# Rotation of queries and keys: one PSUM bank each, four crosswise copies of 256 columns, and a planner that keeps a bank's readers apart

## The chip, the core and the metric

The kernel runs on one core of a Trainium2 chip. The metric is the device time of one execution in microseconds. Three executions of the kernel before took 576.04, 576.35 and 577.06 us.

## The reference

A decoder trunk of two layers works on 256 tokens of 1024 features in float32. Layer 0 is causal block attention with 16 heads of 64 (one block covers all tokens), layer 1 is dilated window attention with 12 heads in three groups. Each is followed by a squared-ReLU MLP of 4096, and each of the four parts ends in a layer norm of `alpha * x + f(x)`. What matters here is how the queries and keys are made:

```python
def apply_rotary(t, cos, sin):
    t1, t2 = jnp.split(t, 2, axis=-1)
    c = cos[None, :, None, :]
    s = sin[None, :, None, :]
    return jnp.concatenate([t1 * c - t2 * s, t2 * c + t1 * s], axis=-1)

...
    qkv = (x @ w_qkv).reshape(B, S, 3, H, dh)
    q = apply_rotary(qkv[:, :, 0], cos, sin) * (dh ** -0.5)
    k = apply_rotary(qkv[:, :, 1], cos, sin)
```

## The kernel before

**Precision and engines.** Every float32 operand is split into a high part (ScalarE, L316) and a low part (VectorE, L321), and a product is three TensorE matmuls: high by high, high by low, low by high. Weights come in tiles of 128 x 1024 through the SP queue into `raw`, and are split into `whi` and `wlo` (`load_w`). A split of 1024 columns takes 1.06 us on ScalarE and 1.22 us on VectorE.

**Pairs of heads.** Two heads fill 128 partitions. For each pair (eight in layer 0, six in layer 1) `proj_qk` projects q and k with 24 matmuls of 256 columns each (`mm_wstat`) into the two halves of one PSUM bank of the tag `acc`. There are four banks `acc` and four `tp`, eight in all. The first two pairs are projected from the staged input (`Stage.mms`, `NFIRST` = 4 projections) while it arrives.

**The rotation** (`rotate`) of such a bank: the feature rows are ordered so that the partner of a row lies 64 partitions away. ScalarE makes two crosswise copies (L544), each of 64 partitions and 512 columns, into the tile `b`. VectorE (L520) multiplies the bank by the cosines into `a`, multiplies `b` by the signed sines, and adds: three instructions of 512 columns. Then q is split into `qhi` and `qlo`, and k into `khi` and `klo` with a head mask (L556, L527).

**After the rotation.** `score` makes the scores in `tp` banks; VectorE masks them and takes the extreme (L591), ScalarE takes the exponential (L601), VectorE scales (L608), TensorE transposes (L615), ScalarE copies the transposed probabilities out of PSUM (`pt`, L623), and TensorE multiplies them with V. Output projection, layer norm and MLP follow.

**The order of the work** comes from a planner (`Plan`). The kernel only lists operations with an engine, a cost and their reads and writes. `order` first works out due times from behind, and then runs all engines forward in estimated time: on each engine it takes, among the operations that can start first, the one that is due first. A buffer of a tag is given to the operations in the order in which the kernel named them; a bank is free when its last operation is done. The resulting order is emitted, and semaphores make each instruction wait for those that it depends on. The emitted program also makes an instruction of ScalarE wait for one of VectorE that reads the same PSUM tile ahead of it in the order, and the other way round. The planner does not know of that wait: reads of one buffer are free of each other in it. A PSUM copy of n columns on ScalarE is put at

```python
    def act(n, aps=0, sbuf=False):
        return n / 1200 + (0.093 if sbuf else 0.055) + 0.093 * aps
```

and the crosswise copies at `act(512) + 0.1`; VectorE's products at `n / 960 + 0.07`.

Of the kernel before, what the change touches and what calls it, by code (L numbers as in the profile page):

```python
# [68 lines left out]
class Buf:  # L69


    def __init__(self, pool, shape, dtype, tag, name):
        self.pool, self.shape, self.dtype, self.tag, self.name = pool, shape, dtype, tag, name
        self.real = None
        self.state = {}
        self.left = 0
        self.held = False

    @property
    def t(self):  # L80
# [9 lines left out]
class Plan:  # L90
# [47 lines left out]
    def order(self):  # L138
        clock = {e: BEGIN[e] for e in ("PE", "SP")}
        bus = 0.0  # L140
        for o in self.ops:
            t = max([clock.get(o.eng, 0.0)] + [p.end + latency(p, o) for p in o.preds])
            o.end = t + o.cost
            if o.eng in clock:
                clock[o.eng] = o.end
            if o.xfer:
                bus = o.end = landed(t, bus, o.xfer)
            o.due = t - o.ahead if o.eng == "PE" else None
        t = clock["PE"]
        for o in reversed(self.ops):  # L150
            for q in o.succs:
                d = q.due - o.cost - latency(o, q)
                o.due = d if o.due is None else min(o.due, d)
            if o.due is None:
                o.due = t - o.early
        engines = sorted({o.eng for o in self.ops})
        free = {e: BEGIN[e] for e in engines}
        bus = 0.0
        cand = {e: [] for e in engines}
        slots = {tag: [0.0] * cap for tag, cap in self.caps.items()}  # L160
        done = []
        for o in self.ops:
            o.wait = len(o.preds)
            o.ready = 0.0
            if not o.wait:
                cand[o.eng].append(o)

        loads = [o for o in self.ops if o.eng == "SP"]

        def start_of(o):  # L170
            s = max(o.ready, free[o.eng])
            need = {}
            for b in o.bufs:
                if not b.held:
                    need.setdefault(b.tag, []).append(b)
            for tag, bs in need.items():
                q = self.queue[tag]
                spare = 0
                if {id(b) for b in q[: len(bs)]} != {id(b) for b in bs}:
                    if tag not in LOOSE:  # L180
                        return None
                    spare = 1
                if len(slots[tag]) < len(bs) + spare:
                    return None
                s = max(s, sorted(slots[tag])[len(bs) - 1])
            return s

        total = len(self.ops)
        while len(done) < total:
            best = None  # L190
            for e in engines:
                lst = [(start_of(o), o) for o in cand[e] if e != "SP" or o is loads[0]]
                lst = [x for x in lst if x[0] is not None]
                if not lst:
                    continue
                first = min(s for s, _ in lst)
                s, o = min((x for x in lst if x[0] <= first), key=lambda x: (x[1].due, x[1].n))
                if e in PATIENT:
                    worst = PATIENT[e]
                    now, ready = s, o  # L200
                    for s2, o2 in lst:
                        if now < s2 < now + ready.cost and o2.due < ready.due:
                            waits = max(s2 - o2.due, s2 + o2.cost - ready.due)
                            runs = max(now - ready.due, now + ready.cost - o2.due)
                            if runs - waits > worst:
                                worst, s, o = runs - waits, s2, o2
                if best is None or s < best[0]:
                    best = (s, o)
            assert best is not None
            s, o = best  # L210
            cand[o.eng].remove(o)
            if o.eng == "SP":
                loads.pop(0)
            for b in o.bufs:
                if not b.held:
                    slots[b.tag].remove(min(slots[b.tag]))
                    self.queue[b.tag].remove(b)
                    b.held = True
            cost = o.cost * 2 if o.eng == "PE" and s < PE_COLD else o.cost
            free[o.eng] = s + cost  # L220
            o.end = s + cost
            if o.xfer:
                bus = o.end = landed(s, bus, o.xfer)
            done.append((s, o.n, o))
            for b in o.bufs:
                b.left -= 1
                b.last = max(getattr(b, "last", 0.0), o.end + (PE_OUT if o.eng == "PE" else LAT))
                if not b.left:
                    slots[b.tag].append(b.last)
            for q in o.succs:  # L230
                q.wait -= 1
                q.ready = max(q.ready, o.end + latency(o, q))
                if not q.wait:
                    cand[q.eng].append(q)
        done.sort(key=lambda x: x[:2])
        return [o for _, _, o in done]
# [7 lines left out]


LOOSE = ("tp",)


LAYOUT = (
# [6 lines left out]
def tile_trunk(  # L256
# [87 lines left out]
    class Stage:  # L344
# [40 lines left out]
        def mms(self, ps, j):  # L385
            kt, hi, lo = self.kt, self.hi, self.lo
            c = slice(self.col(j), self.col(j) + P)
            i = (kt, self.part(j))
            last = kt == KT - 1 and j % 2 == 1
            for w, p, start, stop in ((hi, 0, kt == 0 and j % 2 == 0, False), (hi, 1, False, False), (lo, 0, False, last)):  # L390
                op(
                    "PE", 0.12,
                    lambda w=w, p=p, start=start, stop=stop: mm(
                        ps.t[:, j % 2 * S : j % 2 * S + S], w.t[:, c], xs[kt // 4].t[:, kt % 4, p, :], start, stop
                    ),
                    [(w, i)] + [(xs[kt // 4], (p, kt, m)) for m in range(2)], [ps],
                )
# [47 lines left out]
    def xk(kt, ms):  # L445
        return [(xs[kt // 4], (part, kt, m)) for part in range(2) for m in ms]

    def mm_wstat(ps, w, c0):
        def go_hi(kt):
            for part in range(2):  # L450
                mm(ps.t[:, c0 : c0 + S], w.hi.t[:, kt * P : (kt + 1) * P], xs[kt // 4].t[:, kt % 4, part, :], kt + part == 0, False)

        def go_lo(kt):
            mm(ps.t[:, c0 : c0 + S], w.lo.t[:, kt * P : (kt + 1) * P], xs[kt // 4].t[:, kt % 4, 0, :], False, kt == KT - 1)

        for kt in range(KT):
            op("PE", 0.24, lambda kt=kt: go_hi(kt), [(w.hi, 0)] + xk(kt, (0, 1)), [ps])
# [72 lines left out]
    def rotate(ps, ropet):  # L530
# [1 line left out]
        a = mk([P, 512], F32, "ta", 4)  # L532
        b = mk([P, 512], F32, "ta", 4)

        def pair(ap):
            return ap.rearrange("p (i s) -> p i s", i=2)

        def table(i):
            return ropet.t[:, i, :].unsqueeze(1).to_broadcast([P, 2, S])

        for h in range(2):
            op(
                "ACT", act(512) + 0.1,
                lambda h=h: nc.scalar.activation(b.t[64 * h : 64 * h + 64, :], ps.t[64 - 64 * h : 128 - 64 * h, :], AF.Copy),  # L544
                [ps], [(b, h)],
            )
        tt(512, lambda: pair(a.t), lambda: pair(ps.t), lambda: table(0), ALU.mult, [ps, ropet], [a])
        tt(512, lambda: pair(b.t), lambda: pair(b.t), lambda: table(1), ALU.mult, [b, ropet], [b])
        tt(512, lambda: a.t, lambda: a.t, lambda: b.t, ALU.add, [a, b], [a], ADD_ENG)
        q = mk([P, S], F32R, "qhi", 2), mk([P, S], F32R, "qlo", 2)  # L550
        split(S, lambda: a.t[:, :S], lambda: q[0].t, lambda: q[1].t, [a], [q[0]], [q[1]], sbuf=True)
        hi, lo = mk([P, 2, S], F32R, "khi", 2), mk([P, 2, S], F32R, "klo", 2)
        for h in range(2):
            op(
                "ACT", act(S, 1, True),
                lambda h=h: nc.scalar.activation(hi.t[:, h, :], a.t[:, S:], AF.Copy, scale=hm.t[:, h : h + 1]),  # L556
                [a, hm], [(hi, h)],
            )
            stt(
                S, 1, lambda h=h: lo.t[:, h, :], lambda: a.t[:, S:], lambda h=h: hm.t[:, h : h + 1],  # L560
                lambda h=h: f32(hi.t[:, h, :]), ALU.mult, ALU.subtract, [a, hm, (hi, h)], [(lo, h)],
            )
        return q, (hi, lo)

    def proj_qk(ws):
        ps = psum("acc")
        for i, w in enumerate(ws):
            mm_wstat(ps, w, i * S)
        return ps

    first_ps = [psum("acc") for _ in range(NFIRST // 2)]
    for st in stages:
        for j in range(NFIRST):
            st.mms(first_ps[j // 2], j)

    def score(ps, q, k, qc, kc, off=0):
        (qhi, qlo), (khi, klo) = q, k
# [268 lines left out]
    def layer0(between):  # L846
# [48 lines left out]

        def project(p):
            if 2 * p < NFIRST:
                return rotate(first_ps[p], ropes[0])
            return rotate(proj_qk([load_w(wqk0[2 * p + i - NFIRST]) for i in range(2)]), ropes[0])

        qk, sm = {}, {}
# [214 lines left out]
```

## Time and profile before

| | |
|---|---|
| median of three executions | 576.35 us |
| profiled execution | 576.27 us |
| its span, first to last instruction | 574.5 us |
| granted TensorE clock, mean | 0.997 |
| busy: TensorE matmul, VectorE, ScalarE | 561.4, 418.9, 313.8 us |
| layer 0 attention, its output and the norm | about 0 to 127 us |
| MLP 0 | about 127 to 312 us |
| layer 1 attention, its output and the norm | about 312 to 394 us |
| MLP 1 and the last norm | about 394 to 574.5 us |

In the profile's rows L12 is line 12 of the kernel; `a<-b` names output and inputs. PE is TensorE, ACT is ScalarE, DVE is VectorE. A row of a timeline has the start, the time and the instruction, and in brackets how long its engine had been idle and what released it. A line of a group ends with the busy time in us, the mean of one instruction in ns, and the idle time ahead of such instructions.

### The profile page before, as it was taken

The numbers are of one execution on the slowest core, as the hardware profiler recorded it, in microseconds if no ns is written. First come the engines' busy times: TensorE is split into PE (matmuls) and PEld (weight loads), VectorE is DVE, ScalarE is ACT, GpSimd is POOL, SyncE is SP. The second block draws the span as 40 slices with busy tenths as digits, with TensorE's granted clock in tenths as the row PEclk, the third lists the DMA queues.
The fourth block names the chain that finished last, engine by engine and source line by source line (L and its number), as shares of the span: only waits on it lengthen the run. The fifth ranks groups of instructions, "written<-read, shape, count | busy, mean of one in ns | idle before, by whom it ended". The sixth has DMA issues, their size and how long they took to land.

```text
span 574.5 us, 8588 instructions
## 1 busy us (share of the span) xinstructions
PE 561.4 (98%) x3234; PEld 486.1 (85%) x3234; DVE 418.9 (73%) x729; ACT 313.8 (55%) x529; POOL 8.4 (1%) x13
## 2 busy tenths in 40 slices
PE   8999999999999999999999999999999999999994
PEld 7898898788888888888888997878888888888884
DVE  5898879798775675675678698878966756756644
ACT  6887878456554554455533586844754544544400
POOL 0000000010000000000000000000000000000000
PEclk9999999999999999999999999999999999999998
DMA  8676753627877565555526534534888655655101
GB/s 323 222 242 210 245 184 111 193 83 242 266 274 241 186 212 185 186 189 182 189 80 176 215 129 136 177 111 139 266 261 252 210 187 177 194 186 181 37 1 73
DMA packets 30282, 105.61 MB, mean 184 GB/s; under 512 B 3489, under 2 KB 4257, under 8 KB 30241
## 3 DMA queue, kind: packets, MB, share of 16 engines
q1 hardware_dynamic: 30240, 105.07, 55.8%
q8 instruction: 25, 0.41, 0.3%
q14 instruction: 17, 0.13, 0.1%
HBM read 104.01 MB, written 1.05 MB: 183 GB/s over the span
## 4 chain that ended last, share of the span: by engine, by line
PE 87%; DMA 4%; ACT 4%; DVE 3%; issue 1%; SPq 0%; DVEq 0%; ACTq 0%
PE acc L325 49%; PE tp L325 36%; DMA raw<-in_wv_dram 2%; PE tp L615 2%; ACT whi L316 1%; DVE wlo L321 1%; ACT ta L544 1%; DVE ta L520 1%; DMA raw<-in_wqk_dram 1%; DMA raw<-in_xw_dram 1%; ACT sc L601 0%; DVE tok L527 0%; DVE klo L527 0%; ACT pt L623 0%; ACT khi L556 0%
## 5 line engine op out<-in xcount | busy, mean ns | idle before, releaser
L321 DVE TENSOR_TENSOR wlo<-raw,whi 128x1024 fp32r<-128x1024 f32 (+2 forms) x185 | 222.0, 1206 | 91.4 <-ACT whi L316 91.0
L316 ACT ACTIVATE whi<-raw 128x1024 fp32r<-128x1024 f32 (+2 forms) x184 | 191.0, 1047 | 147.8 <-PE tp L325 69.9
L325 PE MATMUL acc<-whi,ahi 128*128 128x512 f32 (+1 forms) x312 | 119.5, 383 | 0.0
L325 PE MATMUL acc<-wlo,ahi 128*128 128x512 f32 (+1 forms) x312 | 117.3, 380 | 0.0
L325 PE MATMUL tp<-xs,whi 128*128 128x512 f32 x448 | 112.0, 392 | 0.0
L325 PE MATMUL acc<-whi,alo 128*128 128x512 f32 (+1 forms) x312 | 100.7, 379 | 0.0
L325 PEld LDWEIGHTS tp<-xs,whi 128*128 128x128 f32 x448 | 81.1, 189 | 14.9
L325 PEld LDWEIGHTS acc<-whi,ahi 128*128 128x128 f32 x312 | 58.7, 188 | 11.3 <-issue 0.9
L325 PEld LDWEIGHTS acc<-wlo,ahi 128*128 128x128 f32 x312 | 58.7, 188 | 10.4
L325 PE MATMUL acc<-xs,whi 128*128 128x256 f32 x448 | 65.1, 287 | 0.9 <-ACT xs L316 0.6
L325 PEld LDWEIGHTS acc<-whi,alo 128*128 128x128 f32 x312 | 57.1, 188 | 10.5
L325 PEld LDWEIGHTS tp<-xs,wlo 128*128 128x128 f32 x448 | 61.0, 190 | 4.2
L325 PE MATMUL tp<-xs,wlo 128*128 128x256 f32 x448 | 62.6, 283 | 0.0
L325 PEld LDWEIGHTS acc<-xs,whi 128*128 128x128 f32 x448 | 58.6, 192 | 3.0 <-ACT xs L316 1.1
L316 ACT ACTIVATE ahi<-ta 128x256 fp32r<-128x256 f32 x56 | 22.8, 407 | 27.6 <-DVE ta L527 27.5
L325 PE MATMUL acc<-xs,wlo 128*128 128x256 f32 x224 | 36.5, 284 | 0.0
L325 PEld LDWEIGHTS acc<-xs,wlo 128*128 128x128 f32 x224 | 31.0, 192 | 0.7 <-issue 0.7
L325 PE MATMUL acc<-whi,xs 128*128 128x512 f32 (+1 forms) x112 | 28.2, 362 | 0.0
L321 DVE TENSOR_TENSOR alo<-ta,ahi 128x256 fp32r<-128x256 f32 x56 | 23.4, 421 | 6.2 <-ACT ahi L316 6.2
L520 DVE TENSOR_TENSOR ta<-tp,ta 128x256 f32<-128x256 f32 x56 | 23.5, 420 | 5.8 <-ACT ta L769 5.8
L769 ACT ACTIVATE ta<-tp 128x256 f32<-128x256 f32 x56 | 21.0, 375 | 9.3 <-PE tp L325 9.3
L544 ACT ACTIVATE ta<-acc 64x512 f32<-64x512 f32 x28 | 16.6, 593 | 17.4 <-DVE ta L520 11.2
(85 smaller groups left out, 531.8 us busy)
## 6 DMA issues: line engine op xcount, KB each, us to landing
raw<-in_win_dram SPq DMA_DIRECT2D x64, 512.0 KB, 4.3
raw<-in_wout_dram SPq DMA_DIRECT2D x64, 512.0 KB, 4.2
raw<-in_wqk_dram SPq DMA_DIRECT2D x24, 512.0 KB, 4.3
raw<-in_wo_dram SPq DMA_DIRECT2D x14, 512.0 KB, 3.4
raw<-in_wv_dram SPq DMA_DIRECT2D x8, 512.0 KB, 6.7
g<-in_lng_dram SPq DMA_DIRECT2D x4, 512.0 KB, 5.8
b<-in_lnb_dram SPq DMA_DIRECT2D x4, 512.0 KB, 7.8
raw<-in_wv1a_dram SPq DMA_DIRECT2D x4, 512.0 KB, 3.3
```

The costliest lines, as they stand in the source:

```text
L316: op("ACT", act(n, sbuf=sbuf), lambda: nc.scalar.activation(hi(), src(), AF.Copy), r, whi)
L321: lambda: nc.vector.tensor_tensor(lo(), src(), f32(hi()), op=ALU.subtract), list(r) + list(whi), wlo,
L325: nc.tensor.matmul(out_ap, lhsT, rhs, start=start, stop=stop)
L520: op("DVE", dve(n) + extra, lambda: nc.vector.tensor_tensor(out_ap(), a(), b(), op=alu), r, w)
L544: lambda h=h: nc.scalar.activation(b.t[64 * h : 64 * h + 64, :], ps.t[64 - 64 * h : 128 - 64 * h, :], AF.Copy),
L615: nc.tensor.transpose(ps.t[:, c : c + P], src(), ident.t)
L769: op("ACT", act(S), lambda: nc.scalar.activation(u(), ps.t[:, S:], AF.Copy), [ps], uk)
```

## The change

q and k of a pair get a bank of their own: `proj_qk` returns two banks, and the first projections take four banks instead of two. `rotate` makes four crosswise copies of 64 partitions and 256 columns instead of two of 512, and six VectorE instructions of 256 columns instead of three of 512, with dependencies that keep q and k apart. The copies are entered at `act(256)`, without the 0.1. The planner notes the last reader of a buffer, and an operation of another engine that touches a buffer of the tags `tp` or `acc` does not start before that reader's end. The matmuls, the DMAs and everything after the rotation are the same; the order of all engines in the two attention stages is planned anew.

```diff
@@ Plan.order
             for b in o.bufs:
                 if not b.held:
                     need.setdefault(b.tag, []).append(b)
+                elif b.tag in BANKS and o.eng != "PE" and b.reader and b.reader.eng != o.eng:
+                    s = max(s, b.reader.end + latency(b.reader, o))
...
             for b in o.bufs:
+                if o.eng != "PE":
+                    b.reader = o
                 b.left -= 1
...
+BANKS = ("tp", "acc")
@@ rotate
-        for h in range(2):
-            op(
-                "ACT", act(512) + 0.1,
-                lambda h=h: nc.scalar.activation(b.t[64 * h : 64 * h + 64, :], ps.t[64 - 64 * h : 128 - 64 * h, :], AF.Copy),
-                [ps], [(b, h)],
-            )
-        tt(512, lambda: pair(a.t), lambda: pair(ps.t), lambda: table(0), ALU.mult, [ps, ropet], [a])
-        tt(512, lambda: pair(b.t), lambda: pair(b.t), lambda: table(1), ALU.mult, [b, ropet], [b])
-        tt(512, lambda: a.t, lambda: a.t, lambda: b.t, ALU.add, [a, b], [a], ADD_ENG)
+        for i in range(2):
+            for h in range(2):
+                op(
+                    "ACT", act(S),
+                    lambda i=i, h=h: nc.scalar.activation(
+                        cols(b, i)[64 * h : 64 * h + 64], ps[i].t[64 - 64 * h : 128 - 64 * h, :S], AF.Copy
+                    ),
+                    [ps[i]], [(b, (i, h))],
+                )
+        for i in range(2):
+            tt(S, lambda i=i: cols(a, i), lambda i=i: ps[i].t[:, :S], lambda: ropet.t[:, 0, :], ALU.mult,
+               [ps[i], ropet], [(a, i)])
+        for i in range(2):
+            k = [(b, (i, h)) for h in range(2)]
+            tt(S, lambda i=i: cols(b, i), lambda i=i: cols(b, i), lambda: ropet.t[:, 1, :], ALU.mult, k + [ropet], k)
+            tt(S, lambda i=i: cols(a, i), lambda i=i: cols(a, i), lambda i=i: cols(b, i), ALU.add, k + [(a, i)], [(a, i)],
+               ADD_ENG)
...
     def proj_qk(ws):
-        ps = psum("acc")
-        for i, w in enumerate(ws):
-            mm_wstat(ps, w, i * S)
-        return ps
+        pair = []
+        for w in ws:
+            pair.append(psum("acc"))
+            mm_wstat(pair[-1], w)
+        return pair
 
-    first_ps = [psum("acc") for _ in range(NFIRST // 2)]
+    first_ps = [psum("acc") for _ in range(NFIRST)]
     for st in stages:
-        for j in range(NFIRST):
-            st.mms(first_ps[j // 2], j)
+        for j, ps in enumerate(first_ps):
+            st.mms(ps, j)
```

More of the change, by code (lines that the diff above doesn't have):

```diff
@@ L77, in __init__ @@
         self.held = False
+        self.reader = None
     @property
@@ L388, in mms @@
             i = (kt, self.part(j))
-            last = kt == KT - 1 and j % 2 == 1
-            for w, p, start, stop in ((hi, 0, kt == 0 and j % 2 == 0, False), (hi, 1, False, False), (lo, 0, False, last)):
+            for w, p, start, stop in ((hi, 0, kt == 0, False), (hi, 1, False, False), (lo, 0, False, kt == KT - 1)):
                 op(
@@ L393, in mms @@
                     lambda w=w, p=p, start=start, stop=stop: mm(
-                        ps.t[:, j % 2 * S : j % 2 * S + S], w.t[:, c], xs[kt // 4].t[:, kt % 4, p, :], start, stop
+                        ps.t[:, :S], w.t[:, c], xs[kt // 4].t[:, kt % 4, p, :], start, stop
                     ),
@@ L446, in xk, with mm_wstat @@
         return [(xs[kt // 4], (part, kt, m)) for part in range(2) for m in ms]
-    def mm_wstat(ps, w, c0):
+    def mm_wstat(ps, w):
         def go_hi(kt):
             for part in range(2):
-                mm(ps.t[:, c0 : c0 + S], w.hi.t[:, kt * P : (kt + 1) * P], xs[kt // 4].t[:, kt % 4, part, :], kt + part == 0, False)
+                mm(ps.t[:, :S], w.hi.t[:, kt * P : (kt + 1) * P], xs[kt // 4].t[:, kt % 4, part, :], kt + part == 0, False)
         def go_lo(kt):
-            mm(ps.t[:, c0 : c0 + S], w.lo.t[:, kt * P : (kt + 1) * P], xs[kt // 4].t[:, kt % 4, 0, :], False, kt == KT - 1)
+            mm(ps.t[:, :S], w.lo.t[:, kt * P : (kt + 1) * P], xs[kt // 4].t[:, kt % 4, 0, :], False, kt == KT - 1)
         for kt in range(KT):
@@ L533, in rotate, with cols @@
         b = mk([P, 512], F32, "ta", 4)
[L535 to L539, printed above, removed]
-        for h in range(2):
-            op(
-                "ACT", act(512) + 0.1,
-                lambda h=h: nc.scalar.activation(b.t[64 * h : 64 * h + 64, :], ps.t[64 - 64 * h : 128 - 64 * h, :], AF.Copy),
-                [ps], [(b, h)],
-            )
-        tt(512, lambda: pair(a.t), lambda: pair(ps.t), lambda: table(0), ALU.mult, [ps, ropet], [a])
-        tt(512, lambda: pair(b.t), lambda: pair(b.t), lambda: table(1), ALU.mult, [b, ropet], [b])
-        tt(512, lambda: a.t, lambda: a.t, lambda: b.t, ALU.add, [a, b], [a], ADD_ENG)
+        def cols(t, i):
+            return t.t[:, i * S : (i + 1) * S]
+        for i in range(2):
[15 more added lines that the diff above has]
+               ADD_ENG)
         q = mk([P, S], F32R, "qhi", 2), mk([P, S], F32R, "qlo", 2)
-        split(S, lambda: a.t[:, :S], lambda: q[0].t, lambda: q[1].t, [a], [q[0]], [q[1]], sbuf=True)
+        split(S, lambda: a.t[:, :S], lambda: q[0].t, lambda: q[1].t, [(a, 0)], [q[0]], [q[1]], sbuf=True)
         hi, lo = mk([P, 2, S], F32R, "khi", 2), mk([P, 2, S], F32R, "klo", 2)
@@ L556, in rotate @@
                 lambda h=h: nc.scalar.activation(hi.t[:, h, :], a.t[:, S:], AF.Copy, scale=hm.t[:, h : h + 1]),
-                [a, hm], [(hi, h)],
+                [(a, 1), hm], [(hi, h)],
             )
@@ L560, in rotate @@
                 S, 1, lambda h=h: lo.t[:, h, :], lambda: a.t[:, S:], lambda h=h: hm.t[:, h : h + 1],
-                lambda h=h: f32(hi.t[:, h, :]), ALU.mult, ALU.subtract, [a, hm, (hi, h)], [(lo, h)],
+                lambda h=h: f32(hi.t[:, h, :]), ALU.mult, ALU.subtract, [(a, 1), hm, (hi, h)], [(lo, h)],
             )
@@ L897, in project @@
             if 2 * p < NFIRST:
-                return rotate(first_ps[p], ropes[0])
+                return rotate(first_ps[2 * p : 2 * p + 2], ropes[0])
             return rotate(proj_qk([load_w(wqk0[2 * p + i - NFIRST]) for i in range(2)]), ropes[0])
```

## The prediction

> **What bounds the kernel now.** I read the busy times first, then the waits, then the timelines of TensorE and ScalarE around each wait of TensorE.
>
> ```profile
> PE 561.4 (98%) x3234; PEld 486.1 (85%) x3234; DVE 418.9 (73%) x729; ACT 313.8 (55%) x529; POOL 8.4 (1%) x13
> PE tp L615 <- ACT pt L623: 2.6, 3, 1.3
> PE tp L615 <- DVE mx L591: 0.3, 1, 0.3
> PE tp L325 <- ACT xs L316: 0.6, 2, 0.3
> ACT ta L544 <- DVE ta L520: 11.2, 12, 2.7
> DVE ta L520 <- ACT ta L544: 11.8, 14, 3.6
> ```
>
> TensorE is busy for 561.4 of 574.5 us, and the change neither adds nor removes a matmul. So whatever it gains has to come out of the gaps of TensorE. The waits of TensorE (who waited for whom: us in total, times, longest) name few: three waits for a copy of transposed probabilities (2.6 us together), one for a mask step on VectorE (0.3), two after the layer norms (0.6, which the change does not touch). On the other side stands the rotation: ScalarE's crosswise copies (L544) and VectorE's cosine product (L520) wait for each other for over 11 us on each engine. Here are the four gaps that lie behind rotations, and a fifth at the start:
>
> ```profile
> 7.32 0.38 PE L325 MATMUL acc<-xs,whi 128*128 128x256 f32 x1 [0.26 <-DVE xs L321]
> 44.80 1.91 PE L325 MATMUL acc<-xs,whi 128*128 128x256 f32 x14
> 47.67 0.44 PE L615 MATMUL tp<-ident,sc 128*128 128x128 f32 x2 [0.96 <-ACT pt L623]
> 61.24 0.84 PE L615 MATMUL tp<-ident,sc 128*128 128x128 f32 x6 [0.31 <-DVE mx L591]
> 93.82 0.44 PE L615 MATMUL tp<-ident,sc 128*128 128x128 f32 x2 [0.33 <-ACT pt L623]
> 346.35 0.72 PE L325 MATMUL acc<-xs,whi 128*128 128x256 f32 x4
> 348.40 0.65 PE L615 MATMUL tp<-ident,sc 128*128 128x128 f32 x4 [1.33 <-ACT pt L623]
> ```
>
> A row gives the start, the time, and in brackets the idle time before it with its releaser. The gaps sum to 0.26 + 0.96 + 0.31 + 0.33 + 1.33 = 3.19 us. What ScalarE does ahead of three of them:
>
> ```profile
> 44.10 0.59 ACT L544 ACTIVATE ta<-acc 64x512 f32<-64x512 f32 x1
> 45.46 0.59 ACT L544 ACTIVATE ta<-acc 64x512 f32<-64x512 f32 x1 [0.76 <-DVE ta L520]
> 46.07 1.06 ACT L316 ACTIVATE whi<-raw 128x1024 fp32r<-128x1024 f32 x1
> 47.04 0.58 ACT L623 ACTIVATE pt<-tp 128x512 f32<-128x512 f32 x1
> ...
> 92.06 0.59 ACT L544 ACTIVATE ta<-acc 64x512 f32<-64x512 f32 x1 [0.76 <-DVE ta L520]
> ...
> 345.78 0.60 ACT L544 ACTIVATE ta<-acc 64x512 f32<-64x512 f32 x1
> 347.13 0.59 ACT L544 ACTIVATE ta<-acc 64x512 f32<-64x512 f32 x1 [0.76 <-DVE ta L520]
> 347.75 1.09 ACT L623 ACTIVATE pt<-tp 128x512 f32<-128x512 f32 x2
> ```
>
> Each time the second copy stands 0.76 us behind VectorE's product of the same bank, and the copy of probabilities that TensorE waits for stands behind it in ScalarE's queue. The program keeps the two readers of a bank apart; the planner did not know of that, and so it put copy, product, copy.
>
> **The change, part by part.** Prices first:
>
> ```profile
> L544 ACT ACTIVATE ta<-acc 64x512 f32<-64x512 f32 x28 | 16.6, 593 | 17.4 <-DVE ta L520 11.2 <-PE acc L325 5.8
> L769 ACT ACTIVATE ta<-tp 128x256 f32<-128x256 f32 x56 | 21.0, 375 | 9.3 <-PE tp L325 9.3
> L520 DVE TENSOR_TENSOR ta<-acc,ropet 128x512 f32<-128x512 f32 x14 | 9.6, 689 | 9.9 <-ACT ta L544 8.6 <-PE acc L325 1.4
> L520 DVE TENSOR_TENSOR ta<-tp,ta 128x256 f32<-128x256 f32 x56 | 23.5, 420 | 5.8 <-ACT ta L769 5.8
> 36.18 1.04 ACT L316 ACTIVATE whi<-raw 128x1024 fp32r<-128x1024 f32 x1
> 37.13 0.84 ACT L623 ACTIVATE pt<-tp 128x512 f32<-128x512 f32 x2
> 37.99 1.20 ACT L544 ACTIVATE ta<-acc 64x512 f32<-64x512 f32 x2
> ```
>
> *ScalarE.* A crosswise copy of 512 columns takes 593 ns, and two in a row take 1.20 us: they do not overlap, nor do they overlap with what stands before them (37.13 + 0.84 = 37.97, start at 37.99). A PSUM copy of 256 columns takes 375 ns (L769). Four crosswise ones therefore take 4 x 0.40 = 1.6 us, against 1.2 before: +0.4 us per rotation. Where the 0.76 us wait goes, a rotation holds ScalarE 0.36 us less in sum. If the quarter copies do overlap, as other pairs on this engine do (two probability copies of 512 and 256 columns take 0.84 us, not 0.60 + 0.37), four take about 4 x 0.29 = 1.16 us. I take 1.6, because the L544 rows are the nearest, and keep 1.16 for the range. The Trainium skill has a rule on this ("ScalarE: Activation LUTs", section "What ACT_TABLE_LOAD costs"): an instruction without pointer operands costs 186 ns and 0.833 ns per column, and neighbours overlap by about 93 ns. By it four copies would take an estimated 4 x 0.31 = 1.2 us. The L544 rows contradict its overlap for this shape, and no run yet shows the quarter.
>
> *VectorE.* Three instructions of 512 columns (0.69 us each, 2.07) become six of 256 (0.42 each, 2.52): +0.45 us per rotation, +6.3 over the fourteen. It is covered as long as VectorE has free time in the stage (rival two). The q half can be rotated while k is still being projected, and k's last sum then comes after three instructions of 256 rather than of 512 behind k's copies, so no score should be late.
>
> *PSUM.* A projection pair now takes two of the four acc banks instead of one.
>
> ```profile
> 17.35 1.06 ACT L316 ACTIVATE whi<-raw 128x1024 fp32r<-128x1024 f32 x1 [0.18 <-DMA raw<-in_wv_dram]
> 22.73 3.79 PE L325 MATMUL acc<-whi,xs 128*128 128x512 f32 x16
> 30.25 2.08 PE L325 MATMUL acc<-xs,whi 128*128 128x256 f32 x16
> 50.47 2.08 PE L325 MATMUL acc<-xs,whi 128*128 128x256 f32 x16
> 52.39 1.12 PE L325 MATMUL acc<-xs,wlo 128*128 128x256 f32 x8
> ```
>
> Sixteen matmuls of 256 columns start within 1.92 us (52.39 - 50.47), 0.12 each, so a pair of 48 takes 5.8 us, and the next pair but one needs the banks at the earliest 5.8 us after a pair is done. The copies that end at 37.99 + 1.20 = 39.2 read a pair that TensorE completed at 36.0 (48 matmuls from 30.25): 3.2 us. That leaves 2.6 us, so I cost the ring at nothing; if it were late, the projections would wait in TensorE's queue with all behind them. At the start all four acc banks are taken by the first two pairs, and the second half of V (22.73) needs the first one's bank. In the changed order ScalarE reads that bank just ahead of V's fourth weight split (17.35 to 18.41 now), and VectorE soon after it, some 3 us before the need. No DMA moves: the list on SP stays as it was.
>
> *A new wait.* In the changed order ScalarE's copies of a half usually stand behind VectorE's cosine product of that half. Behind them in ScalarE's queue are the exponentials and the probability copies, for which TensorE waits. The worst place is the third pair:
>
> ```profile
> 33.94 0.42 DVE L591 CUSTOM_DVE_ANT_0 sc<-tp,m 128x256 f32<-128x256 f32 x1
> ...
> 36.58 1.44 PE L325 MATMUL acc<-xs,whi 128*128 128x256 f32 x10
> 37.95 0.87 PE L325 MATMUL tp<-pt,v 128*64 128x256 f32 x8
> ```
>
> VectorE comes free for the q product at 33.94; ScalarE can copy from 34.3. Two copies (0.8), three exponentials (0.5, 0.5, 0.4), q's split (0.3) and the k copies (0.8) bring the probability copy from 37.13 to 37.65 and its end to 38.25, where TensorE now takes it at 37.95. Cost **+0.3 us** (0 if copies overlap, 0.6 if VectorE is a product later).
>
> *The gaps, one by one.* At 7.32 the changed program issues the high products of the other projections before the low ones; with three of 0.12 us at hand most of the 0.26 is filled: **-0.2** (0 to 0.26). At 47.67: the way from the first copy to the probability copy takes 2.94 us now (44.10 to 47.04); in the changed order it is four copies and one exponential, 1.6 + 0.5 = 2.1, starting no later. So the release comes about 1 us earlier (0.84 and some 0.2 from the start), at 46.65, while TensorE, 0.3 late from above and with four matmuls (0.48) fewer ahead of the step, arrives at 46.71 + 0.3 - 0.48 = 46.5. About 0.1 stays: of 0.96 I take **-0.8** (0 to 0.96). At 61.24 TensorE waits for a bank that the mask step must read; VectorE lost time twice to this rotation:
>
> ```profile
> 54.24 0.69 DVE L520 TENSOR_TENSOR ta<-acc,ropet 128x512 f32<-128x512 f32 x1 [0.82 <-ACT ta L544]
> 55.59 0.69 DVE L520 TENSOR_TENSOR ta<-ta,ropet 128x512 f32<-128x512 f32 x1 [0.66 <-ACT ta L544]
> ```
>
> These 1.48 us exceed the added 0.45 and the gap: **-0.3**. At 93.82 the transposes stand behind twelve output matmuls instead of four, 1.8 us later at 0.23 each (3.79 us for sixteen at 22.73), and the 0.76 is gone: **-0.3**.
>
> ```profile
> 342.86 1.12 PE L325 MATMUL acc<-xs,wlo 128*128 128x256 f32 x8
> ```
>
> At 348.40 copies, wait and probability copy fill 345.78 to 348.35; in the changed order the q copies are done before k is projected and two k copies (0.8), a weight split (1.0) and the probability copy (0.6) follow k's last matmul, which ends at 342.86 + 1.12 = 344.0; the first of the two cannot start before about 344.9, since a weight split (1.0) stands ahead of it: 347.3. TensorE, which meets the step with the same number of matmuls around it, gains **-1.0** (0 to 1.33).
>
> Sum: -0.2 + 0.3 - 0.8 - 0.3 - 0.3 - 1.0 = -2.3 us. The order of the whole attention stages changes, and new gaps of the size of the small ones seen (0.3) are likely; I allow one: **-2.0 us**. The profiled execution took 576.27 us (its span is 574.5); the median of the three runs is 576.35, 0.08 above. So 576.27 - 2.0 = **574.3 us**.
>
> **Rivals.** *One: the gaps move instead of closing.* The planner puts a quarter copy at 256/1200 + 0.055 = 0.27 us where the rows say 0.40. That is 0.5 us per rotation that it does not know, two thirds of the 0.76 that it does not know now. It also places transposes earlier than before (four matmuls at 47.67). If a gap shrinks only by the third, 0.96 + 0.31 + 0.33 + 1.33 gives 1.0 us, less 0.3 for the new wait: 575.6. Speaks for it: the gaps of today are exactly such errors of the plan. Against: the added time stands at fewer places ahead of a probability copy.
>
> *Two: VectorE becomes the bound between 17 and 60 us*, where four rotations fall:
>
> ```profile
> 17.00:60.00 43.00, 42.04 (x273) 37.21 (x272) 38.63 (x84) 34.90 (x73) 0.00 (x0) 1.00 0.67 213
> ```
>
> The third number is VectorE: 38.63 us busy of 43. The change adds 4 x 0.45 = 1.8 us there. If it has to stand in line with the weight splits that TensorE needs, and the waits of VectorE for ScalarE (0.82 and 0.66 above) come back in other places, all of it arrives at TensorE: 576.27 + 1.8 = 578.1, slower. It decides once less than 1.8 of VectorE's 4.4 free us is free for it. Against it: part of that free time is the waiting for ScalarE, which the change removes, and instructions of 256 columns back to back start closer than 0.42.
>
> *Three: the quarter copies overlap*, 0.29 us each. Then the plan's cost is right, the new 0.3 and my allowance of 0.3 go, and the remainders at 47.67 and 348.40 too (0.1 and 0.3): 576.27 - 3.0 = 573.3. The overlap that the Trainium skill states ("ScalarE: Activation LUTs", as above) would lead to this case. Against: the L544 rows.
>
> *Four: nothing changes that TensorE sees*, because copies and products still wait for each other half by half: 576.3.
>
> **How the numbers follow.** About 0.2% (1.15 us) is what a measurement of this kernel can tell from no change: faster means under 575.2, slower over 577.5. Chances: forecast 0.50, one 0.18, two 0.15, three 0.12, four 0.05. The forecast's own range is 573.2 to 575.2. Faster 0.62, same 0.23, slower 0.15. The range runs from 572.6 (all five gaps closed with the fixed cost around them, 3.2 + 0.5) to 577.4, which leaves out rival two and little else.
>
> **What would show it.** Right: copies L544 of 64x256 at about 0.38 us and 0.40 apart; waits of L544 for L520 well under 11.2 us; TensorE's waits for the probability copy down from 2.6 to about 1 us; a new one near 38 us. Wrong: waits of TensorE for L316, L321 or the score operands between 17 and 60 us, or waits of the projections for a bank, and a busy time of TensorE other than about 561.

## The result and the profile after

The changed kernel takes 574.15 us (median of six executions, 573.51 to 574.90) against 576.21 for the kernel before: a ratio of 0.9962 with a 95% interval of 0.9949 to 0.9975. Its profiled execution took 574.22 us with a span of 572.5. Both kernels' TensorE work is the same, so the 2 us come out of its gaps. The busy line of the page after, then the waits of TensorE, ScalarE and VectorE that answer to those of before (us in total, times, longest):

```profile
PE 561.6 (98%) x3234; PEld 487.1 (85%) x3234; DVE 422.6 (74%) x771; ACT 320.6 (56%) x557; POOL 8.4 (1%) x13
```

```profile
PE tp L627 <- ACT pt L635: 1.1, 1, 1.1
PE acc L332 <- ACT xs L323: 0.3, 1, 0.3
PE tp L332 <- ACT pt L635: 0.2, 1, 0.2
...
ACT ta L548 <- DVE ta L526: 9.8, 10, 1.8
...
DVE ta L526 <- ACT ta L548: 3.9, 10, 0.9
```

TensorE's wait for the transposes behind a probability copy (L627 for L635, formerly L615 for L623) fell from three times and 2.6 us to once and 1.1. ScalarE's wait for the cosine product, though, hardly fell: 9.8 us against 11.2. What became shorter is VectorE's wait for the copies, 3.9 against 11.8. TensorE's gaps in the timeline after:

```profile
38.71 0.87 PE L332 MATMUL tp<-pt,v 128*64 128x256 f32 x8 [0.23 <-ACT pt L635]
46.93 0.44 PE L627 MATMUL tp<-ident,sc 128*128 128x128 f32 x2
60.51 0.81 PE L627 MATMUL tp<-ident,sc 128*128 128x128 f32 x6
347.03 0.66 PE L627 MATMUL tp<-ident,sc 128*128 128x128 f32 x4 [1.07 <-ACT pt L635]
```

The transposes that stood behind gaps at 47.67 and 61.24 now start with no idle time ahead of them, and there is none behind the rotation near 93. The small new wait is there, at 38.71. The gap that was at 348.40 is still a gap, 1.07 us instead of 1.33. ScalarE ahead of the first and the last of these places:

```profile
34.67 0.77 ACT L548 ACTIVATE ta<-acc 64x256 f32<-64x256 f32 x2 [1.75 <-DVE ta L526]
...
37.27 0.77 ACT L548 ACTIVATE ta<-acc 64x256 f32<-64x256 f32 x2
38.06 0.87 ACT L635 ACTIVATE pt<-tp 128x512 f32<-128x512 f32 x2
...
44.19 1.56 ACT L548 ACTIVATE ta<-acc 64x256 f32<-64x256 f32 x4
...
342.76 0.77 ACT L548 ACTIVATE ta<-acc 64x256 f32<-64x256 f32 x2
343.56 1.06 ACT L323 ACTIVATE whi<-raw 128x1024 fp32r<-128x1024 f32 x1
344.64 0.77 ACT L548 ACTIVATE ta<-acc 64x256 f32<-64x256 f32 x2
345.44 1.06 ACT L323 ACTIVATE whi<-raw 128x1024 fp32r<-128x1024 f32 x1
346.40 1.06 ACT L635 ACTIVATE pt<-tp 128x512 f32<-128x512 f32 x2
```

From 342.76 on, ScalarE is never idle: two pairs of copies and two weight splits fill 3.64 us, and the probability copy comes last in the line. Where the time went, stage by stage, is read from the starts of the same matmuls in the two timelines (the kernel before first; between two marks both have the same number of matmuls, but for a record or so):

```profile
17.26 2.00 PE L325 MATMUL tp<-whi,xs 128*128 128x512 f32 x8
43.40 0.40 PE L325 MATMUL tp<-khi,qhi 128*128 128x512 f32 x1
53.35 0.40 PE L325 MATMUL tp<-khi,qhi 128*128 128x512 f32 x1
126.37 1.04 PE L615 MATMUL tp<-ident,tok 128*128 128x128 f32 x8
304.89 1.03 PE L615 MATMUL tp<-ident,tok 128*128 128x128 f32 x8
391.92 1.04 PE L615 MATMUL tp<-ident,tok 128*128 128x128 f32 x8
```

```profile
17.73 1.55 PE L332 MATMUL tp<-whi,xs 128*128 128x512 f32 x6
44.17 0.40 PE L332 MATMUL tp<-khi,qhi 128*128 128x512 f32 x1
53.09 0.40 PE L332 MATMUL tp<-khi,qhi 128*128 128x512 f32 x1
125.23 1.03 PE L627 MATMUL tp<-ident,tok 128*128 128x128 f32 x8
303.73 1.04 PE L627 MATMUL tp<-ident,tok 128*128 128x128 f32 x8
389.89 1.04 PE L627 MATMUL tp<-ident,tok 128*128 128x128 f32 x8
```

The differences, after less before, are +0.47, +0.77, -0.26, -1.14, -1.16 and -2.03. So the start lost 0.47, the stretch with the new wait 0.30; the gap at 47.67 gave 1.03, the rest of layer 0's attention 0.88, MLP 0 0.02, layer 1's attention 0.87. MLP 1 is the same.

### The profile page after: what moved, and what is told of

It is laid out like the page before. It is cut to its first block, busy times and chain, and to the rows that moved or that the text cites. A ratio compares the mean times of both kernels' runs of the same rounds, so it can differ in the third digit from the quotient of the medians.

```text
span 572.5 us, 8665 instructions
## 1 busy us (share of the span) xinstructions
PE 561.6 (98%) x3234; PEld 487.1 (85%) x3234; DVE 422.6 (74%) x771; ACT 320.6 (56%) x557; POOL 8.4 (1%) x13
## 4 chain that ended last, share of the span: by engine, by line
PE 91%; ACT 3%; DMA 2%; DVE 2%; SPq 0%; issue 0%; DVEq 0%
PE acc L332 51%; PE tp L332 37%; PE tp L627 2%; DMA raw<-in_wv_dram 1%; DMA g<-in_xw_dram 1%; DVE wlo L328 1%; ACT whi L323 1%; ACT ta L548 1%; ACT sc L613 1%; DVE tok L533 0%; SPq L319 0%; ACT khi L567 0%; DVE ta L526 0%; DVE sc L603 0%; ACT ta L791 0%
## 5 line engine op out<-in xcount | busy, mean ns | idle before, releaser
L526 DVE TENSOR_TENSOR ta<-tp,ta 128x256 f32<-128x256 f32 x56 | 23.5, 419 | 10.0 <-ACT ta L781 10.0
L548 ACT ACTIVATE ta<-acc 64x256 f32<-64x256 f32 x56 | 21.2, 379 | 10.7 <-DVE ta L526 9.8
```

The source lines that it names most:

```text
L526: op("DVE", dve(n) + extra, lambda: nc.vector.tensor_tensor(out_ap(), a(), b(), op=alu), r, w)
L548: lambda i=i, h=h: nc.scalar.activation(cols(b, i)[64 * h : 64 * h + 64], ps[i].t[64 - 64 * h : 128 - 64 * h, :S], AF.Copy),
```

## The experiments

Theory A: the gain is that the planner knows of the wait between the readers of a bank and no longer puts probability copies behind it. Rival B: it is the separate banks. Each run below is given beside runs of the kernel before on the same chip (576.40, 576.51 and 576.59 us in the three groups).

**The planner's rule alone.** In the kernel before, only this is added to the planner (and the note of each buffer's last reader); rotation and banks stay as they were:

```diff
+                elif b.tag in BANKS and o.eng != "PE" and b.reader and b.reader.eng != o.eng:
+                    s = max(s, b.reader.end + latency(b.reader, o))
```

> The kernel before with the planner's rule on banks alone: two copies of 512 columns, one bank for q and k, three products and sums of 512, as before. Theory A (the planner's knowledge makes the gain): the planner now sees the 0.76 us that the second copy stands behind the cosine product, puts other work of ScalarE there or the copies side by side, and the gaps at 47.67 (0.96 us) and 348.40 (1.33 us) shrink by over half: 574.3 to 575.2 us, and ScalarE's waits for L520 fall from 11.2 us to under 4. Theory B (separate banks make the gain, the rule only keeps the plan in step with them): the rule only writes down a wait that is there anyway, the gaps move, 575.9 to 576.8 us. I give A 0.55.

Measured 572.28 us, ratio 0.9931 (0.9917 to 0.9944): faster than the changed kernel, and more than A expected. Planned with the rule for the `acc` banks alone, every engine's order comes out as with both tags, and with the rule for the `tp` banks alone as in the kernel before (both were planned only, not run), so it is the rotation's banks that the rule is about. The waits and a part of ScalarE's timeline in this run:

```profile
ACT ta L551 <- DVE ta L527: 12.3, 7, 4.9
...
DVE ta L527 <- ACT ta L551: 2.7, 5, 1.3
```

```profile
44.22 0.60 ACT L630 ACTIVATE pt<-tp 128x512 f32<-128x512 f32 x1 [1.28 <-PE tp L622]
44.71 1.05 ACT L323 ACTIVATE whi<-raw 128x1024 fp32r<-128x1024 f32 x1
45.66 0.38 ACT L630 ACTIVATE pt<-tp 128x256 f32<-128x256 f32 x1
46.06 1.20 ACT L551 ACTIVATE ta<-acc 64x512 f32<-64x512 f32 x2
```

ScalarE's waits for the product did not fall to under 4 us: they are 12.3, more than before, and yet TensorE's timeline has no gap of 0.2 us or more left behind the start in either attention stage, besides the 0.30 us behind each layer norm that the kernel before has too. At this place the probability copies now stand ahead of the rotation's copies, and both copies stand together, behind the product. At the place of the gap of 1.33 us the probability copies still follow the rotation's, but there, too, these stand together (343.40) and nothing stalls between them. A wait that the plan knows of costs nothing here; waits that it did not know of cost 4 us.

**The wait taken away, the order kept.** That reading needs the counter-proof: the order of before on every engine, but without the wait. The cosine product reads a table in place of the bank; the q and k in the cosine term are left out.

```diff
-        tt(512, lambda: pair(a.t), lambda: pair(ps.t), lambda: table(0), ALU.mult, [ps, ropet], [a])
+        tt(512, lambda: pair(a.t), lambda: table(1), lambda: table(0), ALU.mult, [ps, ropet], [a])
```

> The kernel before, every engine in the same order, but the cosine product takes the sine table in place of the projection's bank (left out: q and k in the cosine term), so that no copy can wait for that product. Theory A (the gain is that ScalarE no longer stands 0.76 us ahead of the probability copies): 572.3 to 573.3 us, as the rule alone brings, and the waits at 47.67, 93.82 and 348.40 go. Rival F (the order itself must change; the stall is only where the lateness shows): 575 to 576.5 us.

Measured 572.24 us, ratio 0.9929 (0.9915 to 0.9943), the same as the rule alone. TensorE at the place of the gap of 0.96 us, and ScalarE ahead of it:

```profile
45.40 1.91 PE L325 MATMUL acc<-xs,whi 128*128 128x256 f32 x14
47.16 0.38 PE L615 MATMUL tp<-ident,sc 128*128 128x128 f32 x2
```

```profile
44.20 1.20 ACT L544 ACTIVATE ta<-acc 64x512 f32<-64x512 f32 x2 [0.32 <-PE acc L325]
45.42 1.06 ACT L316 ACTIVATE whi<-raw 128x1024 fp32r<-128x1024 f32 x1
46.39 0.58 ACT L623 ACTIVATE pt<-tp 128x512 f32<-128x512 f32 x1
```

The two copies follow each other, and the gap is gone, though in the two traces the instructions of every engine follow each other in the same order. So F falls, and the price of the unplanned waits comes to 576.59 - 572.24 = 4.35 us. (VectorE's product, too, waits for no copy and no projection in this run, so the number holds both directions of the wait, and the one wait of 1.4 us that the product had for a projection.) The Trainium skill ("PSUM — Partial Sum Buffer", section "PSUM bank collisions raise a hardware error") says why such readers have to be kept apart: two engines that access one bank in one quadrant of partitions at the same time mostly get wrong data, reads against reads included, and it is the software that must order them. No run here lets them overlap; what the runs show is the price of the order.

**The banks without the rule.** The changed kernel with `BANKS = ()`.

> The changed kernel without the planner's rule: q and k in a bank each, four copies of 256, but the planner doesn't know that a copy and the cosine product of a half can't read together. Theory A: the plan puts copy and product of one half at the same time again, the copies stall 0.42 us behind a product in most of the fourteen rotations, and about half of the gain of 2 us goes: 575.0 to 575.8 us. Theory B (separate banks make the gain): 574.0 to 574.6 us, since the worst stall of a copy is only 0.42 us, not 0.76, and q's half is out of the way before k's.

Measured 578.36 us, ratio 1.0035 (1.0022 to 1.0047): slower than the kernel before, outside what either theory gave. In its trace product and copies wait for each other more often than before, though for less time in all (7.5 us in 14 waits against 11.2 in 12, 10.1 in 18 against 11.8 in 14):

```profile
ACT ta L548 <- DVE ta L526: 7.5, 14, 1.3
...
DVE ta L526 <- ACT ta L548: 10.1, 18, 2.3
```

TensorE's largest gaps lie behind rotations again:

```profile
48.04 0.41 PE L627 MATMUL tp<-ident,sc 128*128 128x128 f32 x2 [0.93 <-DVE mx L603]
...
349.50 0.66 PE L627 MATMUL tp<-ident,sc 128*128 128x128 f32 x4 [1.14 <-ACT pt L635]
...
359.30 0.63 PE L627 MATMUL tp<-ident,sc 128*128 128x128 f32 x4 [0.93 <-DVE alo L328]
```

The last of them waits for a split on VectorE that stands behind a product of layer 1's last rotation. B falls as the cause of the gain: separate banks without the rule, at the price of the change, lose 2 us. But then the changed kernel, at 574.15, gives back 1.9 us of what its rule brings. The next runs ask why.

**The real price of a copy.** The plan puts a quarter copy at 0.27 us; the groups of the trace after say 0.38, and four in a row (44.19 above) take 1.56, 0.39 each:

```profile
L548 ACT ACTIVATE ta<-acc 64x256 f32<-64x256 f32 x56 | 21.2, 379 | 10.7 <-DVE ta L526 9.8
```

```diff
-                    "ACT", act(S),
+                    "ACT", act(S) + 0.12,
```

> The changed kernel with a crosswise copy priced in the plan at 0.39 us, as the trace has it (379 ns), in place of 0.27. Theory C (the price error of 0.12 us a copy, 0.5 us a rotation, keeps the rest of the gaps open): the wait at 38.71 (0.23 us) and the one at 347.03 (1.07 us) lose half or more together, 573.3 to 573.7 us. Rival D (the gap at 347.03 comes from two weight splits of 1.06 us and the copies that stand ahead of the probability copy for their due times, whatever a copy costs): 573.9 to 574.6 us, with small gaps at other places.

Measured 571.99 us, ratio 0.9925 (0.9913 to 0.9938): C holds, and by more than it gave. Both gaps are gone. ScalarE at the place of the gap at 347.03:

```profile
340.21 2.00 ACT L323 ACTIVATE whi<-raw 128x1024 fp32r<-128x1024 f32 x2
342.23 1.57 ACT L548 ACTIVATE ta<-acc 64x256 f32<-64x256 f32 x4
343.82 1.09 ACT L635 ACTIVATE pt<-tp 128x512 f32<-128x512 f32 x2
```

The two weight splits now stand ahead of the copies instead of between them, and the probability copy comes 2.6 us earlier (343.82 against 346.40), 0.9 of which layer 0 had brought (the transposes of the norm after MLP 0 start at 302.82 here, at 303.73 in the changed kernel). D falls. Three more prices show the shape:

> The changed kernel with a copy priced at 0.51 us, 0.12 too high, where the change has it 0.12 too low. Theory C (a copy that takes longer than planned makes ScalarE late, one that takes less leaves slack): 571.6 to 572.8 us. Rival E (every change of a price gives another plan, and plans scatter by 2 us whatever the price): 573.5 to 576 us as likely as 572, with a new gap of over 0.8 us somewhere.

> The changed kernel with a copy priced at 0.36 us, 0.03 under the measured pitch of 0.39. Theory C (the time follows the price error): 571.8 to 572.6 us. Rival E (plans scatter by a us or more with any price): 573 to 575 us as likely.

> The changed kernel with a copy priced at 0.42 us, 0.03 above the measured pitch. Theory C: 571.8 to 572.6 us, and not above the 573.1 of the price of 0.51. Rival E: 573 to 575 us as likely.

| price of a copy in the plan | us | ratio (95% interval) |
|---|---|---|
| 0.27 (the change) | 574.15 | 0.9962 (0.9949 to 0.9975) |
| 0.36 | 572.36 | 0.9926 (0.9915 to 0.9938) |
| 0.39 (as measured) | 571.99 | 0.9925 (0.9913 to 0.9938) |
| 0.42 | 572.09 | 0.9927 (0.9914 to 0.9941) |
| 0.51 | 573.12 | 0.9945 (0.9933 to 0.9958) |

A valley with its floor around the measured value: C. The three prices around the floor, whose orders differ from each other in some hundreds of rows, agree within 0.4 us, so E falls. A price that is too high costs too, 1.1 us, where C had expected 572.8 at most. Against the profile at 0.39, that at 0.51 is 0.60 us longer in layer 0's attention from V's first matmul to the norm (18.76 to 125.94 us against 17.72 to 124.30) and 0.75 in layer 1's (304.48 to 389.99 against 302.82 to 387.58). It names no wait of TensorE over 0.3 us in these stretches; what makes up the loss stays open.

**The same error in the simple rotation.** Rule alone, with `act(512) - 0.14` in place of `act(512) + 0.1` for the two copies: the same 0.48 us a rotation too low.

> The run with the rule alone (two copies of 512 columns, one bank; 572.28 us), but each copy priced 0.24 us below what it takes, 0.48 us a rotation, which is the error that the changed kernel's four copies bring. Theory C (the price error is what the change loses against the rule alone): 573.8 to 575.2 us, with TensorE waiting for probability copies behind rotations again. Rival D (four quarter copies and six products are themselves too much for the engines; the price matters only through the one gap near 347 us): 572.0 to 572.9 us.

Measured 573.69 us, ratio 0.9953 (0.9940 to 0.9966), 1.4 us above the rule alone: just under C's range and well over D's. Small gaps are back (0.41 us at 61.07, 0.51 at 349.37). The price error costs in both rotations, though 1.4 us here and 2.2 there.

**Quarters in one bank.** The rule, four copies and six VectorE instructions, but q and k in one bank; once with the price of the change, once with the measured one.

> The changed kernel with q and k in one bank, as before the change: four copies of 256 columns, six products and sums of 256, the planner's rule. What is left out against the changed kernel is only the second bank, and with it that q's half can be read while k is projected. Theory B (separate banks make the gain): ScalarE pays 0.4 us and VectorE 0.45 us more per rotation for nothing, and copies and products of both halves stand in one line: 575.8 to 577 us, so slower than the run with the rule alone by 0.3 or more. Theory A (the planner's knowledge makes the gain): as the run with the rule alone, within 0.4 us, 574.4 to 575.4.

> Quarters in one bank with the rule (574.72 us), and each copy priced at 0.39 us as measured. Theory C: it falls to 571.8 to 572.8 us like the changed kernel with that price, so that the second bank is worth under 0.5 us. Theory B (separate banks matter): it stays at 573.5 us or above, since q's half still waits for k's projection and the readers of both halves stand in one line.

Measured 574.72 us (ratio 0.9970, 0.9961 to 0.9979) and 573.79 (0.9953, 0.9939 to 0.9966). With the right price the second bank is worth 573.79 - 571.99 = 1.8 us, so C's estimate for it (under 0.5) falls and B is right in that much; with the wrong price only 0.6 of it shows, within the intervals. Against the rule alone, the finer pieces in one bank cost 573.79 - 572.28 = 1.5 us. That is what the second bank buys back. Its way of doing so is not shown in full: one gap is 0.61 us long and stands at 383.62, where TensorE waits for a split behind the layer norm; the rest is in smaller pieces.

**Banks and price without the rule.**

> Banks apart and copies priced at 0.39 us, but the planner without the rule. Theory A (the rule is needed): copies and products of one half are still put at the same time, each time 0.42 us late, 575 to 577.5 us. Rival (any plan whose costs are right does; the rule adds little once the price is right): 571.8 to 573 us.

Measured 575.92 us, ratio 0.9993 (0.9984 to 1.0001): as A gave. The gap near 348 us is there in full:

```profile
347.95 0.66 PE L627 MATMUL tp<-ident,sc 128*128 128x128 f32 x4 [1.40 <-ACT pt L635]
```

Together (us):

| | without the rule | with the rule | the rule |
|---|---|---|---|
| two copies of 512, one bank | 576.40 | 572.28 | -4.1 |
| four of 256, two banks, priced 0.27 | 578.36 | 574.15 | -4.2 |
| four of 256, two banks, priced 0.39 | 575.92 | 571.99 | -3.9 |

The parts add up (the runs come from groups whose runs of the kernel before lie between 576.21 and 576.51 us). The rule brings about 4 us with each of the three; the wrong price costs 2.2 to 2.4; quarters in two banks, rightly priced, bring 0.3 to 0.5, which the intervals don't tell from nothing. So of the change, the rule gains some 4 us, the price loses 2.2, and the rewritten rotation brings next to nothing. The rule alone and the change with the measured price both beat the two kernels.

## Why the prediction came out right

The forecast was 574.3 and the result 574.15. The mechanism was right: the plan did not know of the wait between a bank's readers, and the gaps behind it shrank once it did. But several terms were off and cancelled, so a distance of 0.15 us is luck. By its own steps:

| step | predicted, us | measured, us |
|---|---|---|
| start, gap at 7.32 | -0.2 | +0.47 in the two profiles, not shown to come from the change (last section) |
| new wait near 38 us | +0.3 | +0.30 (0.23 in its row) |
| gap at 47.67 | -0.8 | -1.03 |
| gaps at 61.24 and 93.82 | -0.6 | -0.88 |
| gap at 348.40 | -1.0 | -0.87 for layer 1's attention; the gap itself -0.26 |
| allowance for new gaps | +0.3 | none of 0.2 us or more besides the new wait |

- *The start.* The gap at 7.32 is gone, but V's first matmul starts no earlier for it: at 17.38 to 17.73 us in the profiles with the new order of the start and at 17.26 to 17.86 in those with the old one, one late profile of each left out. The -0.2 does not show.
- *The copies.* The forecast took no overlap and 0.40 us each; 379 ns and 0.39 apart are the rows. The overlap of rival three does not occur, nor does the estimate of 0.31 us that the Trainium skill ("ScalarE: Activation LUTs", section "What ACT_TABLE_LOAD costs") led to.
- *The gaps of layer 0* were sized by the bracketed idle time, which is too small. Before the gap of 0.96 us, fourteen matmuls start at 44.80 and the next instruction at 47.67: 2.87 us, where 14 x 0.12 = 1.68 were needed, so 1.19 were lost. That made these terms too small by a quarter and more. It also set the lower end of the range too high: 572.6 was to be "all five gaps closed", the five gaps sum to 3.19 us by their brackets, and the run without the wait, which closes them except the start's, gained 4.35.
- *348.40* is the step that failed in its mechanism. The forecast had the q copies done before k was projected, so that k's copies followed k's last matmul by 0.9 us (344.9 against 344.0), behind one weight split. In the trace k's last matmul ends at 341.69 + 1.12 = 342.81:

```profile
341.69 1.12 PE L332 MATMUL acc<-xs,wlo 128*128 128x256 f32 x8
```

  Only about then, at 342.76, do the q copies start; the weight split stands behind them, and k's copies start at 344.64, 1.8 us after that matmul. So the gap shrank by 0.26 us and not by 1.0. The stage's 0.87 came near because it gained another 0.6 us elsewhere, which no term had forecast. With the measured price layer 1's attention took 1.4 us less than in the changed kernel.
- *Waits of L548 for L526 "well under 11.2"* was wrong as a sign: 9.8, and 12.3 in the better run with the rule alone. What counts is who stands behind the wait.
- *Rival one* had the right mechanism for what was left over: the price error of 0.5 us a rotation. It was worth 2.2 us, and did not keep the layer 0 gaps open, so the 575.6 was not reached. *Rival two* did not happen: VectorE rose to 41.18 of 43 us between 17 and 60, and TensorE did not wait for it there.

```profile
17.00:60.00 43.00, 42.77 (x278) 37.90 (x277) 41.18 (x106) 37.12 (x85) 0.00 (x0) 1.00 0.65 219
```

- *What the prediction did not do* is to split the change in two. It named the plan's ignorance of the wait, but costed rule and rotation as one; alone, the rule closes every gap behind a rotation.

## What to carry to other kernels

Where an order is planned from costs, first compare the planner's waits and prices with the trace's rows: a hidden wait of 0.76 us and a price 0.12 us too low cost 4 and 2 us here, more than any rewriting of the instructions gained. A large sum of waits between two engines says little; look at what is queued behind each wait, and whether the plan knew of it. When an instruction is cut into smaller ones, measure the new piece and put its price into the plan in the same change.

## What the hardware showed that was not expected

The start of the kernel differs from execution to execution. The same first matmuls in the same order, before and after:

```profile
4.71 0.64 PE L325 MATMUL acc<-xs,whi 128*128 128x256 f32 x4
5.18 0.40 PE L325 MATMUL acc<-xs,wlo 128*128 128x256 f32 x2
```

```profile
4.74 1.05 PE L332 MATMUL acc<-xs,whi 128*128 128x256 f32 x4
5.59 0.63 PE L332 MATMUL acc<-xs,wlo 128*128 128x256 f32 x2
```

Four matmuls start within 0.47 us (0.12 each) in one and within 0.85 us (0.21 each) in the other. In the run with the rule alone they took 0.86, with the price 0.77. The trace's records of the granted clock fit this: the first of them, of the full clock, begins at 4.66 us in the one profile and at 6.94 in the other, so the four matmuls stand behind it in the one and ahead of it in the other. In the profile of the run that prices the two copies of 512 too low, the records grant half the clock from 7.98 to 11.39 us (the last number but two in this row), and two matmuls take 0.42 us there (8.57 to 8.99), 0.21 each:

```profile
8.00:11.30 3.30, 3.30 (x15) 3.30 (x16) 2.06 (x5) 2.71 (x6) 0.00 (x0) 0.50 1.01 391
```

The Trainium skill ("TensorE: Matmul & The Clock Gate", section "What's actually happening") describes a half-rate phase after the start that ends with a window of time and not with a number of matmuls. The records agree in that their first entry begins anywhere between 4.02 and 6.99 us in the thirteen profiles.

The first matmul of V started between 17.26 and 17.86 us in eleven of the thirteen profiles, and at 18.76 (the price of 0.51) and 19.41 (the run with the half clock) in the two others. There ScalarE's splits of the input waited for DMAs, 2.21 and 1.06 us in the one and 2.08 and 1.42 in the other, where the kernel before waited once, 1.39 us. Each of the two profiles is of the slowest execution of its run: 574.31 us with a median of 573.12, and 575.11 with 573.69. So a few tenths of a microsecond at the start of one profile can't be laid to a change, and the +0.47 in the table is not shown to come from the change.
